# A hybrid GLA / DeltaNet block on Trainium2: the first tiles of the projection rearranged

## The chip, the cores and the metric

The kernel runs on one core of a Trainium2 chip, as one launch. The metric is the device time in microseconds of that launch, the median of several runs. The engines are PE (matmuls, with PEld for its weight loads), DVE, ACT, POOL (GpSimd) and SP, which here only issues DMAs; each has its own queue, worked off in order.

## The reference

One layer with 1024 tokens and a model width of 1024, all float32. A conditioning vector `c` gives six vectors of shift, scale and gate (adaLN); the first two act before the big projection.

```python
mod = silu(c) @ ada_w + ada_b                      # 1024 x 6144
shift1, scale1, gate1, shift2, scale2, gate2 = split(mod, 6)
h = rms_norm(x, pre_mix_w) * (1.0 + scale1) + shift1
proj = h @ w_in                                    # columns for GLA, DeltaNet, merge gates
# DeltaNet branch: d_k = l2_norm(silu(conv(proj[dk]))), beta = sigmoid(proj[beta]),
#                  g = -exp(a_log) * softplus(proj[da] + dt_bias), chunked delta rule
# GLA branch: gk = log_sigmoid(proj[lr] @ w_lr + b_lr) / 16, chunked gated linear attention
merged = sigmoid(m_a) * y_a + sigmoid(m_d) * y_d
x = x + gate1 * rms_norm(merged @ w_out, post_mix_w)
h2 = rms_norm(x, pre_mlp_w) * (1.0 + scale2) + shift2
x = x + gate2 * rms_norm(square(relu(h2 @ mlp_w1)) @ mlp_w2, post_mlp_w)
```

## The kernel before, in words

Activations are kept with channels on partitions: `hH[d]`, `hL[d]` hold channels 128 d to 128 d + 127 of all 1024 tokens. Each float32 operand is split into a high part, rounded to the matmul format, and a low part, the rest. A projection tile of 128 output columns is 8 blocks d times three products (high weight with high h, high with low, low with high) times two halves of 512 tokens: 48 matmuls into one PSUM tile of 1024 columns (pool `pm`, two tiles). A second pool, `pa`, has four banks of 512 columns for everything small.

*Start (lines 135 to 212).* SP's queue loads the eight tiles of x (128 tokens by 1024 channels each) with two small loads behind each one. `x_norm(g)` (186) takes two tiles: ACT squares with a running sum, DVE makes 1/sqrt by 13 small operations, GpSimd multiplies both tiles by it (for the last tile, DVE). The small vectors are transposed by PE into the columns `vcol` and `ccol`.

*adaLN (214 to 300).* `ada_load(p)` brings, for p = 0 to 3, the weight columns of shift and scale that belong to channel blocks 2p and 2p+1, in eight DMAs of 256 KB. The sum over the 1024 rows is shared out: the first `KPE[p]` row blocks go to PE as matmuls with one column (`ada_pe`), the rest to DVE as multiply-adds of 512 columns (`ada_part`; for p = 0 two of the blocks on GpSimd); `ada_fin` closes the sum over partitions on PE, and DVE makes shift `sh1` and scale `am1`. `modulate(p)` (301) writes `hH`, `h` (both on ACT; for p = 3 `h` on DVE) and `hL`, the difference, on DVE for one block and on GpSimd for the other. `xT`, the transposed x, comes from PE transposes, copied out of eight banks for the first four token tiles and four banks at a time for the others.

*First tiles (421 to 470).* Four rounds p: while DVE and ACT make the next two blocks, PE multiplies those that are ready with two weight tiles: the narrow tile (64 columns: low rank, beta and decay inputs, high and low part) and the first key tile of 128 columns. 14 transposes that nobody reads (`WARM`) stand ahead of the first products. From line 177 to the end of `first_tiles` the engines are strict: the class `InOrder` (27) chains each instruction of an engine behind the last one written for it. Outside of that the framework chooses the order by its own estimate of when things are ready.

*Keys (1143 to 1158).* `key_tiles` gives the first key tile and then seven more by `dense_n`, whose weights `splits` (387) prepares one ahead: ACT casts the high part, GpSimd subtracts the low part (engine G in `plan`, 378). For each tile `gdn_k` (622) does convolution, SiLU, transposes, square sums; `gates_small` (496) takes the narrow tile through DRAM and a chain of small operations to the decays; `gdn_D` (651) and `gdn_A` (659) make the decay matrix and the gram products of a head.

*The agenda (332 to 349).* `at(dt, fn)` puts work on a list to be issued dt ticks later; a tick is one of the eight blocks of a tile. The due times are numbers written by hand: transposes of keys 7 ticks after their tile, `gdn_A` 14 behind these.

Of the kernel before, what the change touches and what calls it, by code (L numbers as in the profile page):

```python
# [50 lines left out]
def block_kernel(ctx: ExitStack, tc: tile.TileContext, x, c, ada_w, ada_b, pre_mix_w, post_mix_w,  # L51
# [86 lines left out]
    smalls, o = [], 0  # L138
    for src, n in ((c, 8), (ada_b, 48), (pre_mix_w, 8), (pre_mlp_w, 8), (post_mix_w, 8), (post_mlp_w, 8), (gla_b_lr, 4),
                   (gla_onorm_w, 2), (gdn_onorm_w, 1)):  # L140
        smalls.append((vt[o:o + n, :], src.rearrange("o (r p) -> (o r) p", p=128)))
        o += n
    smalls.append((cvt, conv_w.rearrange("j (r p) -> (j r) p", p=128)))
    smalls += [(wlr[o:o + 16, :], gla_w_lr) for o in (0, 32, 64)]
    xs = []
    for i in range(NT):
        xt = t4(p="x")
        last["ld"] = DMA.dma_start(xt, x[i * 128:(i + 1) * 128, :]).ins
        xs.append(xt)
        for dst, src in smalls[2 * i:2 * i + 2]:  # L150
            with tc.issue_after(last["ld"]):
                last["ld"] = DMA.dma_start(dst, src).ins
# [3 lines left out]
    make_identity(nc, ident)  # L156
    onesR = cp.tile([128, 128], F32R, name="onesR")
# [4 lines left out]
    raw_lba = rp.tile([128, 8, 32], F32, tag="raw", name=nm("raw"))  # L162
# [16 lines left out]

    for e in engines:  # L180
        e.strict = True
# [12 lines left out]

    x_norm(0)
# [10 lines left out]
    x_norm(1)  # L206
    sigmoid(sct, ccl, V)
    V.tensor_mul(sc, ccl, sct)
    x_norm(2)
    x_norm(3)  # L210

# [11 lines left out]

    ada_load(0)
    with tc.issue_after(last["ld"]):
        for (o, c0, n) in ((0, C_LR, 16), (16, C_BETA, 8), (24, C_DA, 8)):
            DMA.dma_start(raw_lba[:, :, o:o + n], w_in[:, c0:c0 + n].rearrange("(k p) c -> p k c", p=128))
        raws0[C_DK] = load_w(w_in, C_DK, 128)
    last["ld"] = last["dma"]
    ada_load(1)  # L230

    KPE = (0, 2, 2, 1)
    WARM = 14
# [9 lines left out]
    def ada_part(p):  # L243

        for k in range(KPE[p], 8):
            r_ = araw[(p, k // 2)][:, k % 2]
            if not p and k < 2:
                a_ = t4((128, 2, 256), p="acc")
                G.tensor_scalar(a_, r_, sc[:, k:k + 1], 1.0, ALU.mult, ALU.mult)
                if k:  # L250
                    G.tensor_tensor(a_, accs[p], a_, ALU.add)
                accs[p] = a_
            elif k == (KPE[p] if p else 2):
# [895 lines left out]
    for h, ps in enumerate(key_tiles()):  # L1149
# [3 lines left out]
        elif h == 1:  # L1153
            next(gs)
# [712 lines left out]
```

## Time and profile before

| | us |
|---|---|
| median of 3 runs (lowest, highest) | 1968.18 (1964.47, 1970.18) |
| the profiled execution | 1963.2 |
| its span | 1961.5 |
| PE busy | 1921.7 |
| DVE, ACT, POOL busy | 1447.3, 801.9, 172.1 |

The page of the profile gives busy times by engine, a chain that ended last, and groups of instructions; the timeline gives single instructions with their start, their duration and, in brackets, how long the engine sat idle before them and what released it. Times in timelines count from the start of the span. All helpers record line 38, so instructions are told by their tiles: `pm` and `pa` are PSUM, `xT`, `hH`, `hL`, `h` the activations, `acc` and `araw` the adaLN sums and weights, `wH`, `wL`, `w`, `wS` weights, `cv` and `si` key convolution and its tanh, `lba` the narrow tile, `gr` the decay matrix.

### The profile page before, as it was taken

The page shows a single profiled execution, that of the slowest core. Times are in us where ns is not written, and L with a number is a line of the kernel's source. Part 1 is how long each engine was busy: PE and PEld are TensorE (multiplying, and loading weights), DVE is VectorE, ACT ScalarE, POOL GpSimd, SP SyncE. Part 2 cuts the span into 40 slices and gives each one's busy share as a digit, 9 for nine tenths or more (in the row PEclk, how much of TensorE's full clock was granted, in tenths as well). Part 3 has the DMA queues.
Part 4 walks back from the last instruction along what each step waited for, and adds up shares of the span by engine and source line. Part 5 has one row for each costly group of instructions (what it writes and reads, how often), then busy time and mean ns, then how long its engine had stood idle before and what let it go on. Part 6 is the DMA issues. An engine that isn't in the chain of part 4 may idle for free.

```text
span 1961.5 us, 26008 instructions
## 1 busy us (share of the span) xinstructions
PE 1921.7 (98%) x9894; PEld 1622.6 (83%) x9894; DVE 1447.3 (74%) x2653; ACT 801.9 (41%) x1427; POOL 172.1 (9%) x120
## 2 busy tenths in 40 slices
PE   5999999999999999999999999999999999999998
PEld 4788888889899888888888888888888888888886
DVE  7867599658769697888787434666668886787887
ACT  5554323342342333333336231247644446343333
POOL 3300100310110100000001110000012220000001
PEclk8999999999999999999999999999999999999999
DMA  9365622423222433333358785244666767452525
GB/s 295 111 211 178 202 101 84 143 65 108 60 70 76 143 111 105 116 117 114 96 162 208 184 192 124 102 131 159 205 216 214 245 228 258 158 204 66 202 97 97
DMA packets 214444, 292.24 MB, mean 149 GB/s; under 512 B 33695, under 2 KB 153966, under 8 KB 214318
## 3 DMA queue, kind: packets, MB, share of 16 engines
q1 hardware_dynamic: 174910, 243.50, 38.1%
q10 hardware_dynamic: 21760, 35.01, 5.0%
q0 software_dynamic: 17648, 12.06, 4.7%
q8 instruction: 78, 1.28, 0.3%
q14 instruction: 48, 0.39, 0.1%
HBM read 215.42 MB, written 75.11 MB: 148 GB/s over the span
## 4 chain that ended last, share of the span: by engine, by line
PE 46%; DVE 3%; DMA 1%; ACT 0%; issue 0%; DVEq 0%; ACTq 0%
PE pa L38 23%; PE pm L38 23%; DVE obT L38 1%; DVE cv L38 0%; DMA sl<-sg_d 0%; DMA os<-oa_d 0%; DVE oL L38 0%; DVE rt L38 0%; DVE si L38 0%; DVE sqt L38 0%; DVE ya L38 0%; DVE rs L38 0%; DVE sqr L38 0%; DVE yg L38 0%; DVE st L38 0%
## 5 line engine op out<-in xcount | busy, mean ns | idle before, releaser
L38 PE MATMUL pm<-hH,wH 128*128 128x512 f32 x1008 | 327.6, 405 | 0.4 <-DVE cv L38 0.4
L38 PE MATMUL pm<-hL,wH 128*128 128x512 f32 x1008 | 314.5, 393 | 0.0
L38 PE MATMUL pm<-hH,wL 128*128 128x512 f32 x1008 | 313.5, 391 | 0.1
L38 PEld LDWEIGHTS pm<-hH,wL 128*128 128x128 f32 x1008 | 189.4, 188 | 41.8 <-DVE wL L38 0.5
L38 PEld LDWEIGHTS pm<-hL,wH 128*128 128x128 f32 x1008 | 189.6, 188 | 40.9
L38 PE MATMUL pa<-w,yH 128*128 128x512 f32 x688 | 212.1, 390 | 0.0
L38 ACT CAST wH<-raw 128x1024 fp32r<-128x1024 f32 x95 | 99.1, 1051 | 270.7 <-PE pm L38 189.1
L38 PEld LDWEIGHTS pm<-hH,wH 128*128 128x128 f32 x1008 | 176.7, 190 | 26.4 <-issue 1.1
L38 DVE TENSOR_TENSOR w<-raw,w 128x512 fp32r<-128x512 f32 (+1 forms) x142 | 123.4, 872 | 49.3 <-ACT w L38 48.5
L38 PEld LDWEIGHTS pa<-w,yH 128*128 128x128 f32 x688 | 129.1, 188 | 27.2 <-DVE ya L38 0.4
L38 ACT CAST w<-raw 128x512 fp32r<-128x512 f32 (+1 forms) x143 | 98.2, 708 | 88.9 <-DVE raw L38 79.8
L38 PE MATMUL pa<-w,yL 128*128 128x512 f32 x344 | 133.9, 389 | 0.0
L38 PE MATMUL pa<-oB,w 128*128 128x512 f32 x480 | 111.4, 390 | 0.0
L38 DVE SCALAR_TENSOR_TENSOR cv<-pm,ccol,cv 128x1023 f32<-128x1023 f32 (+2 forms) x72 | 92.1, 1280 | 24.2 <-ACT cv L38 23.1
L38 DVE TENSOR_TENSOR wL<-raw,wH 128x1024 fp32r<-128x1024 f32 x72 | 88.5, 1236 | 26.9 <-ACT wH L38 26.6
L38 PEld LDWEIGHTS pa<-oB,w 128*128 128x128 f32 x480 | 89.8, 188 | 18.5 <-DVE w L38 0.2
L38 PE MATMUL pa<-oT,w 128*128 128x512 f32 x384 | 90.8, 389 | 0.0
L38 PE MATMUL pm<-oT,w 128*128 128x512 f32 x384 | 90.8, 389 | 0.0
L38 DVE TENSOR_TENSOR ya<-pa,ya 128x512 f32<-128x512 f32 x82 | 55.9, 689 | 43.3 <-PE pa L38 43.3
L38 PEld LDWEIGHTS pa<-oT,w 128*128 128x128 f32 x384 | 72.1, 188 | 14.9
L38 PEld LDWEIGHTS pm<-oT,w 128*128 128x128 f32 x384 | 72.1, 188 | 14.9
L38 PE MATMUL pm<-oH,wH 128*128 128x512 f32 x256 | 80.7, 396 | 0.0
(329 smaller groups left out, 3808.7 us busy)
## 6 DMA issues: line engine op xcount, KB each, us to landing
yL<-y_d SPq DMA_DIRECT2D x53, 512.0 KB
raw<-in_mlp_w_dram SPq DMA_DIRECT2D x23, 1024.0 KB
raw<-in_w_in_dram SPq DMA_DIRECT2D x19, 1024.0 KB
raw<-in_w_in_dram SPq DMA_DIRECT2D x34, 512.0 KB
araw<-in_ada_w_dram SPq DMA_DIRECT2D x32, 512.0 KB
raw<-in_mlp_w_dram SPq DMA_DIRECT2D x18, 512.0 KB
araw<-in_ada_w_dram SPq DMA_DIRECT2D x32, 256.0 KB
sg_d<-sig ACTq DMA_DIRECT2D x16, 512.0 KB
```

What stands on the lines that cost most here:

```text
L38: r = fn(*args, **kw)
```

## The change

- The eight tiles of x are loaded one behind the other on SP's queue; the small loads go to ACT's and GpSimd's queues. Behind x come the key weights (256 columns in place of 128), all adaLN weights, and last the narrow columns.
- The scaling of x: even tiles on DVE, odd tiles on ACT, each group of two ahead of the next squares on ACT. All eight banks serve both halves of the transposes.
- adaLN sums: PE takes 3, 2, 2, 2 row blocks in place of 0, 2, 2, 1, DVE the rest, GpSimd none. `quad` is made at the start.
- `modulate` makes `hH` and `h` on ACT; `low(d)` makes `hL[d]` on DVE alone, one block a round and the last five behind the third round.
- `first_tiles` works on two key tiles at once: `hi(p)` is 16 matmuls with the high part of h (two blocks, two tiles, high and low weight, two halves), `lo(w, d)` two matmuls with the low part. Transposes ahead of the first products: 10.
- The narrow tile follows as `lba_tile`, 32 matmuls and eight ticks, into two banks of `pa`.
- The low weights of the six other key tiles: no engine subtracts; ACT writes the negated high part, and a DMA of GpSimd's queue adds the weights to it.
- Due times: head 0's transposes still 7 ticks behind, head 1's 12; `gdn_A` 20 and 18 ticks behind these for heads 0 and 1; `gdn_D(0)` and `gdn_D(1)` at the third key tile.

```diff
-    def x_norm(g):
+    def x_sq(g):
         for i in (2 * g, 2 * g + 1):
-            A.activation(t4(p="jk"), xs[i], AF.Square, accum_out=ssq[:, i:i + 1])
+            A.activation(xT[i], xs[i], AF.Square, accum_out=ssq[:, i:i + 1])
+
+    def x_root(g):
         v = small(2, "xv")
         V.tensor_scalar(v, ssq[:, 2 * g:2 * g + 2], 1.0 / D, EPS, ALU.mult, ALU.add)
         r = rsqrt(v, 2)
-        for i in range(2):
-            (V if i and g == 3 else G).tensor_scalar(xs[2 * g + i], xs[2 * g + i], r[:, i:i + 1], 1.0, ALU.mult, ALU.mult)
+        V.tensor_scalar(xs[2 * g], xs[2 * g], r[:, 0:1], None, ALU.mult)
+        return r
+    def x_odd(g, r):
+        A.activation(xs[2 * g + 1], xs[2 * g + 1], AF.Copy, scale=r[:, 1:2])
...
+    banks = banks8()
+    x_odd(0, r0)
+    x_tr(0)
+    x_tr(1)
+    x_sq(1)
+    r1 = x_root(1)
...
+    x_odd(1, r1)
+    x_tr(2)
+    x_tr(3)
+    x_sq(2)
+    r2 = x_root(2)
+    x_odd(2, r2)
+    x_sq(3)
+    r3_ = x_root(3)
+    for d in range(8):
+        if d == 5:
+            x_odd(3, r3_)
+        A.copy(xT[d][:, :512], banks[d])
+    banks = banks8()
+    for i in range(4, 8):
+        x_tr(i)
+    wk = []
+    for i in range(2):
+        wk.append([t4((128, 8, 128), F32R, "w0", "wt") for _ in range(2)])
+        A.copy(wk[i][0], raw_k[:, :, i * 128:(i + 1) * 128])
+        V.tensor_tensor(wk[i][1], raw_k[:, :, i * 128:(i + 1) * 128], wk[i][0].bitcast(F32), ALU.subtract)
+    KPE = (3, 2, 2, 2)
...
+    ada_part(0)
     for d in range(8):
-        A.copy(xT[d][:, :512], banks[d])
+        if d % 4 == 3:
+            V.tensor_copy(xT[d][:, 512:], banks[d])
+        else:
+            A.copy(xT[d][:, 512:], banks[d])
...
+    def low(d):
+        hL[d] = t4(dt=F32R, p="hL")
+        V.tensor_tensor(hL[d], hs[d], hH[d].bitcast(F32), ALU.subtract)
...
-    plan = [(w_in, C_DK + 128, 128, 8, G)]
-    plan += [(w_in, C_DK + 256 + j * 256, 256, 8, G) for j in range(3)]
+    plan = [(w_in, C_DK + j * 256, 256, 8, None) for j in range(1, 4)]
...
     def first_tiles():
+        pk = [pmt(), pmt()]
...
+        def hi(p):
+            for d in (2 * p, 2 * p + 1):
+                for w in range(2):
+                    mm(w, 0, d, hH[d], start=(d == 0), stop=False)
+                    mm(w, 1, d, hH[d], start=False, stop=False)
+        def lo(w, d):
+            mm(w, 0, d, hL[d], start=False, stop=(d == 7))
+        ada_pe(0)
+        ada_fin(0)
+        modulate(0)
+        ada_pe(1)
+        warm(WARM)
+        for p in range(1, 4):
+            ada_part(p)
+            hi(p - 1)
+            ada_fin(p)
+            modulate(p)
+            low(p - 1)
+            if p < 3:
+                ada_pe(p + 1)
+                for w in range(2):
+                    lo(w, p - 1)
+        for d in range(3, 8):
+            low(d)
+        for w in range(2):
+            lo(w, 2)
+        hi(3)
+        for w in range(2):
+            for d in range(3, 8):
+                lo(w, d)
...
-    for h, ps in enumerate(key_tiles()):
-        gdn_k(h, ps, 7)
+    gdn_k(0, pk[0], 7, 20)
+    gdn_k(1, pk[1], 12, 18)
+    gs = gates_small(lba_tile())
+    next(gs)
+    for h, ps in enumerate(dense_n(6, h_rhs), 2):
+        gdn_k(h, ps, 7)
+        if h == 2:
+            next(gs)
+            gdn_D(0)
+        gdn_D(h - 1)
```

More of the change, by code (lines that the diff above doesn't have):

```diff
@@ L137, in block_kernel @@
     G.memset(wlr, 0.0)
[L138 to L144, printed above, removed]
     xs = []
@@ L161, in block_kernel @@
     ones = onesR.bitcast(F32)
-    raw_lba = rp.tile([128, 8, 32], F32, tag="raw", name=nm("raw"))
+    for o in (0, 32, 64):
+        G.dma_start(wlr[o:o + 16, :], gla_w_lr)
+    quad = cp.tile([128, 4, 32], F32, name="quad")
+    for a in range(0, 128, 32):
+        V.tensor_copy(quad[a:a + 32], ident[a:a + 32, a:a + 32].unsqueeze(1).to_broadcast([32, 4, 32]))
     vcol = cp.tile([128, 95], F32, name="vcol")
@@ L469, in first_tiles @@
-        for part in "lk":
-            mm(6, 1, part)
-            mm(7, 1, part)
-        for e in engines:
-            e.strict = False
+        V.tensor_tensor(wS[:, :, 32:64], raw_lba, wS[:, :, 0:32].bitcast(F32), ALU.subtract)
+        pl = [pat(), pat()]
+        for k in range(8):
+            for lo in range(2):
+                for hf in range(2):
+                    last["pe"] = T.matmul(pl[hf][:64, :], wS[:, k, :], h_rhs(k, hf, lo), start=(k == 0 and lo == 0),
+                                          stop=(k == 7 and lo == 1)).ins
+            tick()
@@ L474, in first_tiles @@
         sb = t4((64, 1024), p="lba")
         sb2 = t4((64, 1024), p="lb2")
-        A.copy(sb2, pl[0:64, :])
+        for hf in range(2):
+            A.copy(sb2[:, hf * 512:(hf + 1) * 512], pl[hf][0:64, :])
         V.tensor_copy(sb[0:32], sb2[32:64])
-        V.tensor_add(sb[0:32], sb[0:32], sb2[0:32])
-        return sb, pk
+        last["ev"] = V.tensor_add(sb[0:32], sb[0:32], sb2[0:32]).ins
+        return sb
     lrS = t4((96, 1024), F32R, p="lrS")
@@ L585, in block_kernel @@
     ssK = cp.tile([128, 64], F32, name="ssK")
-    quad = cp.tile([128, 4, 32], F32, name="quad")
-    for a in range(0, 128, 32):
-        V.tensor_copy(quad[a:a + 32], ident[a:a + 32, a:a + 32].unsqueeze(1).to_broadcast([32, 4, 32]))
     QT = 18
```

209 lines of the change are left out of this document (71 added, 138 removed).

## The prediction

> **What bounds the kernel now.** I read the page first, then the stretches of 10 us, then the waits of PE after the start, then the timeline of each engine up to 120 us.
>
> ```profile
> span 1961.5 us, 26008 instructions
> PE 1921.7 (98%) x9894; PEld 1622.6 (83%) x9894; DVE 1447.3 (74%) x2653; ACT 801.9 (41%) x1427; POOL 172.1 (9%) x120
> ...
> PE 46%; DVE 3%; DMA 1%; ACT 0%; issue 0%; DVEq 0%; ACTq 0%
> ```
>
> ```profile
> 20.00:30.00 10.00, 6.49 (x27) 4.34 (x26) 9.40 (x20) 5.76 (x12) 7.33 (x6) 0.77 1.01 258
> 30.00:40.00 10.00, 8.07 (x55) 7.35 (x54) 9.66 (x18) 4.83 (x7) 3.08 (x2) 0.84 1.10 351
> 40.00:50.00 10.00, 8.14 (x31) 5.64 (x29) 9.75 (x14) 6.57 (x6) 3.22 (x2) 0.70 1.12 337
> ...
> 70.00:80.00 10.00, 9.78 (x44) 7.76 (x42) 9.90 (x6) 2.91 (x3) 8.11 (x6) 1.00 0.69 216
> 80.00:90.00 10.00, 7.62 (x31) 6.25 (x32) 7.07 (x10) 6.42 (x24) 2.38 (x1) 0.83 0.26 73
> ```
>
> ```profile
> PE pa L38 <- DVE yn L38: 4.9, 5, 1.3
> ```
>
> PE is busy 98% of the span. The columns of the stretches are PE, PEld, DVE, ACT, POOL, then the granted clock, DMA share and GB/s. PE loses time before 60 us, where it idles and its clock is below 1, and between 80 and 90 us, at 0.83. Behind 86 us its largest wait is 4.9 us in all. The change touches only the work up to the last key tile, and the matmuls behind are the same. So its worth is how much earlier or later PE reaches one point of equal work: the start of the third key tile. All that PE must do ahead of it (narrow tile, two key tiles, eight transposes) is the same in both kernels.
>
> ```profile
> 70.10 0.61 PE L38 MATMUL pm<-hH,wH 128*128 128x512 f32 x2
> 70.55 0.62 PE L38 MATMUL pm<-hL,wH 128*128 128x512 f32 x2
> ...
> 82.39 0.66 PE L38 MATMUL pa<-ident,cv 128*128 128x128 f32 x4 [2.60 <-DVE cv L38]
> ...
> 85.62 1.20 PE L38 MATMUL pm<-hH,wH 128*128 128x512 f32 x2
> 86.62 0.76 PE L38 MATMUL pm<-hL,wH 128*128 128x512 f32 x2
> ```
>
> At full clock two matmuls start every 0.45 us, 0.227 us each. The third key tile starts at 85.62. Its first pair takes 1.0 us to the next pair instead of 0.45, so it stands as if it had started at 86.1: that is the mark. Ahead of it PE waited 2.60 us for the activated first key tile, and from 82.39 to 86.62, 4.2 us, it ran at the slow clock.
>
> **The change, part by part.** GpSimd's work is in DVE's way now.
>
> ```profile
> 30.98 0.75 DVE L38 SCALAR_TENSOR_TENSOR acc<-araw,sc,acc 128x512 f32<-128x512 f32 x1
> ...
> 33.64 3.40 DVE L38 COPY quad<-ident 32x128 f32<-32x128 f32 x4
> ...
> 41.10 2.95 DVE L38 SCALAR_TENSOR_TENSOR acc<-araw,sc,acc 128x512 f32<-128x512 f32 x1
> 43.97 1.21 DVE L38 TENSOR_TENSOR hL<-h,hH 128x1024 fp32r<-128x1024 f32 x1
> ```
>
> ```profile
> 41.14 2.36 POOL L38 TENSOR_TENSOR hL<-h,hH 128x1024 fp32r<-128x1024 f32 x1 [4.42 <-ACT h L38]
> ```
>
> The same sum takes 0.75 us alone and 2.95 us beside GpSimd's 2.36 us subtraction. A subtraction on GpSimd therefore costs DVE 2.2 us, and on DVE itself 1.21 us. So moving three of them over gains about 1 us of DVE each, and moving quad ahead frees 3.4 us of DVE before the first shift and scale. Whether that reaches PE is settled by the chain, in seven steps.
>
> *1. x.* ACT now alternates: two squares, the wait for DVE's root, one scaling.
>
> ```profile
> 7.76 1.06 ACT L38 ACTIVATE jk<-x 128x1024 f32<-128x1024 f32 x1 [1.26 <-DMA x<-in_x_dram]
> 8.72 0.19 ACT L38 ACTIVATION_READ_ACCUMULATOR jk<-x 128x1 f32 x1
> ```
>
> ```profile
> 8.94 0.17 DVE L38 TENSOR_SCALAR xv<-ssq 128x2 f32<-128x2 f32 x1 [8.94 <-ACT jk L38]
> ...
> 11.12 0.16 DVE L38 SCALAR_TENSOR_TENSOR rs<-rt,rs 128x2 f32<-128x2 f32 x1
> ```
>
> A square with its sum is 1.15 us. A root is 13 small operations from 8.94 to 11.28, 2.35 us; now it lies beside ACT's next squares, afterwards ACT stands still in it. The scaling I take as 1.06 (a pass of the same size). A group is 2.3 + 2.35 + 1.06 + 0.2 for two handovers = 5.9 us. Loading x ahead brings a tile every 1.5 us (0.52 MB at the 351 GB/s of the second stretch), faster than ACT uses them, so only the first two arrivals count: start at 5.3 as now, 0.4 us for the second tile. The nine small loads on ACT's queue must be issued before 5.3 us; I cost them at nothing, at most 1 us if the issues run longer. Four groups end at 5.7 + 23.6 = 29.3.
>
> *2. Transposes of the second half.*
>
> ```profile
> 19.69 2.05 ACT L38 COPY xT<-pa 128x512 f32<-128x512 f32 x4 [0.15 <-PE pa L38]
> ...
> 33.24 1.06 ACT L38 CAST w<-raw 128x1024 fp32r<-128x1024 f32 x1
> ```
>
> ```profile
> 26.07 6.43 PE L38 MATMUL pa<-ident,x 128*128 128x128 f32 x24 [2.69 <-POOL x L38]
> ...
> 33.56 1.73 PE L38 MATMUL pa<-ident 128*128 128x128 f32 x14
> ```
>
> The fourth pair's squares end at 5.7 + 17.7 + 2.3 = 25.7. Eight copies of 0.52 and the last scaling behind them end at 25.7 + 4.2 + 1.1 = 31.0 on ACT, and only then are all banks free. Some 24 transposes remain. The 24 of before took 6.43 with waits, the 14 at full clock 0.12 each; at half that pace they have 0.215 to 0.24. I take 0.215, 5.2 us: 36.2.
>
> *3. The first shift and scale.* ACT casts both weights, 2.1 us, to 33.1. DVE subtracts twice (1.21, as hL) to 34.3, then runs ada_part(0): 0.47 + 4 x 0.77 = 3.55, to 37.9 (0.77 is the 0.75 with its handover), then the copy that frees the fourth bank. On SP's queue the adaLN blocks of round 0 now come behind x and the 1.05 MB of key weights: 7.35 MB at 351 GB/s are 21 us behind the first bytes at 3 to 4, so 25, and DVE wants them at 34.3: covered by 9 us. Each further round's 2.1 MB take 6 us more, and rounds last 8.
>
> ```profile
> 32.44 1.28 DVE L38 COPY xT<-pa 128x512 f32<-128x512 f32 x2
> ...
> 37.45 0.47 DVE L38 TENSOR_SCALAR acc<-araw,sc 128x512 f32<-128x512 f32 x1
> ```
>
> ```profile
> 44.10 1.05 PE L38 MATMUL pa<-onesR,acc 128*128 128x1 f32 x8 [1.77 <-DVE acc L38]
> ...
> 47.30 1.06 PE L38 MATMUL pm<-hL,wS 128*64 128x512 f32 x2
> 48.15 0.63 PE L38 MATMUL pm<-hL,w 128*128 128x512 f32 x1
> ...
> 49.63 1.84 PE L38 MATMUL pa<-sc,araw 128*128 128x1 f32 x16
> ```
>
> ```profile
> 37.49 2.37 ACT L38 ACTIVATE hH<-xT,sh,am 128x1024 fp32r<-128x1024 f32 x2 [3.20 <-DVE am L38]
> ...
> 45.56 2.37 ACT L38 ACTIVATE hH<-xT,sh,am 128x1024 fp32r<-128x1024 f32 x2 [3.43 <-DVE am L38]
> ```
>
> The copy (0.64) ends at 38.6. PE's column sums ada_pe(0) then need some 20 more records of 0.115 to 0.12, 2.4 us, and the closing sums with DVE's additions 1.5 us (44.10 to 45.56): 42.5. Before, this point is 37.49. So I have the start 5 us later.
>
> *4. First round.* ada_pe(1) 1.84 to 44.3; ten transposes at 0.215 to 46.5; then hi(0), 16 matmuls. PE has had nothing but sums since 36.2, so it starts slow and stays so for the 4.2 us seen above, until 48.5: 4.8 matmuls at 0.425 (two from 47.30 to 48.15), the other 11.2 at 0.227, to 51.0. With the closing 1.5, 52.5.
>
> The row bears on a rule: the 24 transposes at 26.07 had slow clock, and by the stretches the 14 at 33.56, right behind, have 0.12 us each. Transposes count as work here. The Trainium skill, "TensorE: Matmul & The Clock Gate", Part 4, says that a transpose doesn't engage the full clock. By that rule the slow stretch would begin only at 46.5, and the sum would be 1 us more; the trace disagrees.
>
> *5. Rounds two and three.* PE: ada_pe 1.84, four low matmuls 0.9, 16 matmuls 3.63, closing 1.5, handovers 0.15: 8.0 us each, to 68.5. DVE needs 1.21 + 0.47 + 5 x 0.77 = 5.5 beside it, hidden. A round of before took 8.1 (37.49 to 45.56). Its bounds: 7.0 if sums and matmuls overlap by the waits, 9.7 if the clock drops for one 3.4 us stretch.
>
> *6. Low parts last.* After the third round DVE has six subtractions of 1.21 in a row, to 75.8; PE works beside them and ends 12 matmuls, 2.7 us, after the last: 78.5.
>
> *7. Narrow columns behind.* 32 matmuls 7.3 us, eight transposes 1.05: the third key tile at 86.9. Against the mark of 86.1 that is 0.8, say **+1 us**. The narrow matmuls cover the activation of the first key tile, so the 2.60 us wait goes.
>
> Six low parts of weights now come by adding DMA, as those of the branches do.
>
> ```profile
> DMA to landing us min/median/max: 6.7/8.9/15.3
> ```
>
> modulate(3) is four passes of 1.18 (37.49's two in 2.37) and ends at 73.2, the cast and the negation behind it at 75.3; the first DMA lands at 82 to 91 and is needed at 87.8: nothing at the median, 3 us at the longest. ACT pays a pass of 1.06 for each, hidden in a tile of 48 matmuls, 10.9 us.
>
> The profiled run's own time is 1963.2 around its 1961.5 span; +1 gives 1964. The median of three runs shown is 1968.18, so I forecast **1969**. 0.3%, 5.9 us, is about what a measurement of this kernel can tell from no change. Bounds of the steps (clock in step 5, -2 to +3.4; the DMA, 0 to 3; step 4, -2 to +1) leave this case at 1965 to 1976.
>
> **The rivals.**
>
> *The start isn't later (faster).* If ACT's three waits in the roots (7 us) don't reach PE, because x stays paced by its arrival and the copies, the first shift and scale come at 35 instead of 42.5: 7.5 us less, 1961.5. For it: DVE is 9.4 to 9.75 of 10 busy in these stretches and loses GpSimd's interference and quad. Against it: the groups are chained in the engines' fixed order.
>
> *The gates come late (slower).* The narrow tile now stands behind two key tiles.
>
> ```profile
> 72.03 3.31 DVE L38 TENSOR_TENSOR lba<-lba,lb 32x1024 f32<-32x1024 f32 x1
> 75.27 3.90 DVE L38 SCALAR_TENSOR_TENSOR cv<-pm,ccol,cv 128x1023 f32<-128x1023 f32 x3
> ...
> 105.76 3.34 DVE L38 SCALAR_TENSOR_TENSOR gr<-gr,gcC,negmask 128x128 f32<-128x128 f32 x8
> ```
>
> From its sum (75.3) to the first decay (105.8) passed 30.4 us. Afterwards the narrow matmuls end at 85.8, their copies and sums near 90, and 30.4 on is 120; decay (3.3), exponential (1.1) and product (0.75) end at 125; the gram tiles of heads 0 and 1 are due from ticks 28 and 31, 115 to 120. Four PSUM banks then hold, and PE stands 4 to 5 us with a slow clock behind, worth 2: +7 with the sum, 1975. It decides from a chain longer than some 26 us. For it: conv is queued on DVE behind the decay. Against: the due times of heads 0 and 1 were moved back by 6 and 1 ticks.
>
> *The wait at 82 stays.* The first key tile is done at 76.3; a copy and a tanh as passes of 1.1 each, taps 3.9, one tap of the other tile 1.3 and the closing pass of 1.2 end at 84.9; the transposes are due at 84.9. If DVE is behind by 2.6 us, PE waits that and runs slow again: +5, 1973, still no measurable change.
>
> **How the numbers follow.** Forecast 0.42; the wait that stays 0.10; earlier start 0.27; late gates 0.21. So faster 0.27, same 0.52, slower 0.21. The range goes 9 us to both sides, 1960 to 1978: it takes in the middle of both outer cases and leaves out their tails, some 2 in 10. The likeliest case's own is 1965 to 1976.
>
> **What would show it.** In the changed profile ACT's first hH should begin at 42.5 (35 by the faster rival), the next three 8 to 10 us apart, each DVE sum of 512 columns take 0.75, and the third key tile start at 87. PE's waits before 86 us should name the DVE sums and the roots; a wait for gr or the gram tiles between 110 and 130 us would be the slower rival. A first hH before 37 would make the forecast wrong in step 1 or 3.

## The result, and the profile after

The changed kernel takes 1987.42 us (median of 5 runs, 1985.57 to 1988.95). The kernel before, run beside it on the same chip, takes 1964.68 (5 runs, 1963.70 to 1970.18). The ratio is 1.0103, with a 95% interval of 1.0091 to 1.0116: slower by 20 us as the ratio has it, by 22.7 as the medians have it, where the forecast said 1969, 1960 to 1978. The profiled execution took 1987.42, 24.2 more than the 1963.2 of before, which lies under the lowest of these five: differences between the two traces come out a few us too large.

The page of the kernel after, its span and TensorE's busy time:

```profile
span 1985.7 us, 26066 instructions
...
PE 1927.0 (97%) x9922; PEld 1628.3 (82%) x9922; DVE 1432.1 (72%) x2657; ACT 813.9 (41%) x1440; POOL 143.2 (7%) x108
```

The waits of its TensorE (total, how often, the longest):

```profile
PE pa L38 <- DMA vt<-in_gdn_onorm_w_dram: 20.7, 1, 20.7
PE pm L38 <- DVE cv L38: 6.7, 2, 3.9
PE pa L38 <- ACT xT L38: 6.2, 1, 6.2
```

The first wait names a DMA of the small loads, and the second the key convolution, behind the first tiles. These are the two places where the time went. Three points show how much went where:

| | before | after | difference |
|---|---|---|---|
| first hH on ACT | 37.49 | 53.24 | +15.8 |
| third key tile on PE | 86.1 (the mark) | 99.89 | +13.8 |
| first sigmoid of the gates of the merge | 188.5 | 212.2 | +23.7 |

So 13.8 us are lost ahead of the third key tile, another 9.9 between it and the gates of the merge, and nothing to speak of later (23.7 of the 24.2).

**Ahead of the third key tile.** The timeline of ACT in the kernel after; ACTq rows are issues of DMAs from ACT's queue:

```profile
5.54 0.59 ACTq L38 DMA_DIRECT2D vt<-in_c_dram  x1
...
10.36 0.28 ACTq L38 DMA_DIRECT2D vt<-in_pre_mlp_w_dram  x1
13.09 0.28 ACTq L38 DMA_DIRECT2D vt<-in_post_mix_w_dram  x1
14.34 0.28 ACTq L38 DMA_DIRECT2D vt<-in_post_mlp_w_dram  x1
15.65 0.25 ACTq L38 DMA_DIRECT2D vt<-in_gla_b_lr_dram  x1
15.95 0.27 ACTq L38 DMA_DIRECT2D vt<-in_gla_onorm_w_dram  x1
16.25 0.26 ACTq L38 DMA_DIRECT2D vt<-in_gdn_onorm_w_dram  x1
16.56 1.06 ACT L38 ACTIVATE xT<-x 128x1024 f32<-128x1024 f32 x1 [12.74 <-DMA vt<-in_gla_onorm_w_dram]
...
21.22 1.15 ACT L38 ACTIVATE x<-x,rs 128x1024 f32<-128x1024 f32 x1 [2.47 <-DVE rs L38]
...
53.24 2.37 ACT L38 ACTIVATE hH<-xT,sh,am 128x1024 fp32r<-128x1024 f32 x2 [4.90 <-DVE am L38]
63.91 2.38 ACT L38 ACTIVATE hH<-xT,sh,am 128x1024 fp32r<-128x1024 f32 x2 [6.03 <-DVE am L38]
72.78 2.37 ACT L38 ACTIVATE hH<-xT,sh,am 128x1024 fp32r<-128x1024 f32 x2 [4.22 <-DVE am L38]
80.05 2.38 ACT L38 ACTIVATE hH<-xT,sh,am 128x1024 fp32r<-128x1024 f32 x2 [2.63 <-DVE am L38]
```

The nine issues themselves take 0.25 to 0.59 us each, but the first seven go out 1.3 to 2.7 us apart (only the last three follow each other in 0.3 us), and ACT does nothing else until the last one is out. The first square of x starts at 16.56. Before, it starts at 5.35.

The stretches of 10 us of the kernel after (the columns as in the prediction):

```profile
20.00:30.00 10.00, 6.56 (x34) 5.71 (x34) 5.17 (x27) 6.41 (x11) 0.00 (x0) 0.95 0.99 325
30.00:40.00 10.00, 2.12 (x6) 0.75 (x5) 5.49 (x28) 7.48 (x15) 0.00 (x0) 0.50 1.10 348
40.00:50.00 10.00, 8.47 (x46) 7.91 (x46) 7.04 (x9) 5.83 (x10) 0.00 (x0) 0.67 0.83 228
...
70.00:80.00 10.00, 9.92 (x61) 8.67 (x59) 6.63 (x15) 4.65 (x4) 0.00 (x0) 1.00 0.01 2
80.00:90.00 10.00, 8.63 (x38) 7.12 (x39) 7.51 (x9) 9.75 (x10) 2.73 (x5) 1.00 0.14 32
```

DVE, 9.4 to 9.75 of 10 busy before, has 5 to 7 now, and 6.63 against 9.90 between 70 and 80 us. The change did relieve it, and the relief is worth nothing while the chain starts 11 us late.

**Between the third key tile and the gates of the merge.** One stretch from the one point to the other, in the kernel before:

```profile
86.10:188.50 102.40, 101.96 (x521) 85.40 (x520) 67.80 (x120) 53.79 (x170) 7.73 (x5) 1.00 0.59 196
```

and in the kernel after:

```profile
99.89:212.20 112.31, 105.31 (x525) 87.40 (x524) 70.29 (x128) 58.55 (x183) 5.68 (x5) 0.97 0.73 206
```

The matmuls are the same but for a few missing records, but PE stands idle for 7.0 us (112.31 less 105.31) instead of 0.4, and it is busy 3.4 us longer at a mean clock of 0.97: together the 9.9. DVE of the kernel after shows the first idle place:

```profile
131.33 2.60 DVE L38 SCALAR_TENSOR_TENSOR cv<-pm,ccol,cv 128x1023 f32<-128x1023 f32 x2 [2.23 <-ACT cv L38]
138.51 2.19 DVE L38 SCALAR_TENSOR_TENSOR gr<-gr,gcC,negmask 128x128 f32<-128x128 f32 x8 [4.58 <-DMA gr<-gc_d]
140.61 1.28 DVE L38 SCALAR_TENSOR_TENSOR cv<-pm,ccol,cv 128x1021 f32<-128x1021 f32 x1
```

and PE, which needs the convolved tile's PSUM:

```profile
142.03 1.19 PE L38 MATMUL pm<-hH,wH 128*128 128x512 f32 x2 [3.94 <-DVE cv L38]
...
160.90 0.70 PE L38 MATMUL pm<-hH,wH 128*128 128x512 f32 x2 [2.75 <-DVE cv L38]
```

Two taps of a convolution are done. Then the first decay stands at the head of DVE's queue and waits 4.58 us for its load of `gr`, with the third tap behind it and PE behind that. The narrow sum ends at 108.9 and the first decay starts at 138.5, 29.6 us later; before it was 30.4. The gates come 32.7 us later than before (138.5 against 105.8), the key tiles only 13.8.

The wait has a second side, the load itself. SP issues it in the kernel before and in the kernel after at

```profile
99.67 0.36 SPq L653 DMA_DIRECT2D gr<-gc_d  x1
```

```profile
128.79 0.35 SPq L667 DMA_DIRECT2D gr<-gc_d  x1
```

Before, the decay at 105.76 doesn't wait, so that its load took at most 6.1 us; now it takes until 138.5, 9.7 us. For most of that time the DMA engines have next to nothing to do (the last columns, 0.04 busy and 17 GB/s):

```profile
130.00:136.00 6.00, 6.00 (x36) 5.27 (x35) 2.56 (x2) 3.68 (x7) 1.54 (x1) 1.00 0.04 17
```

With the 6.1 us of before it would have landed at 134.9, and DVE, free from 133.9 on, would have waited 1 us and not 4.58 (an estimate from these rows). The slow load doesn't come with the new order: where a first decay waits for its load, in old orders (e2, e9, e12, e18) and new ones, it took 8.8 to 10.3 us, once 6.7 (e4). What makes it slow isn't shown.

The second wait of PE, 2.75 us at 160.90, comes by ACT's queue: DVE has stood idle for 5.0 us when the first tap reaches it at 156.84, and ACT had the exponentials of two decays and a held store ahead of that tap.

### The profile page after: what moved, and what is told of

Read it like the earlier page. It is cut to its first block, busy times and chain, and to the rows that moved or that the text cites. A ratio compares the mean times of both kernels' runs of the same rounds, so it can differ in the third digit from the quotient of the medians.

```text
span 1985.7 us, 26066 instructions
## 1 busy us (share of the span) xinstructions
PE 1927.0 (97%) x9922; PEld 1628.3 (82%) x9922; DVE 1432.1 (72%) x2657; ACT 813.9 (41%) x1440; POOL 143.2 (7%) x108
## 5 line engine op out<-in xcount | busy, mean ns | idle before, releaser
L38 PE MATMUL pm<-hH,wH 128*128 128x512 f32 x992 | 322.6, 405 | 6.7 <-DVE cv L38 6.7
L38 PE MATMUL pm<-hL,wH 128*128 128x512 f32 x992 | 309.5, 392 | 0.0
L38 PE MATMUL pm<-hH,wL 128*128 128x512 f32 x992 | 309.0, 392 | 0.1
L38 PEld LDWEIGHTS pm<-hL,wH 128*128 128x128 f32 x992 | 186.5, 188 | 40.6
```

The source lines that it names most:

```text
L38: r = fn(*args, **kw)
```

## The experiments

Each kernel ran beside the kernel before on one chip; the ratio is to that. The theory was that two things cost the time: the small loads on ACT's queue, and gates that come late against the key tiles. The rivals are named with each run. Kernels that ran on different chips are compared by their ratios. One trace is good to some 2 us: six kernels with the same code ahead of the first hH (after, e3, e4, e5, e10, e16) have it between 52.3 and 54.2.

| kernel | ratio to before (95%) | first hH | third key tile | first decay | first sigmoid |
|---|---|---|---|---|---|
| before | | 37.5 | 86.1 | 105.8 | 188.5 |
| after | 1.0103 (1.0091 to 1.0116) | 53.2 | 99.9 | 138.5 | 212.2 |
| e1 small loads on SP | 1.0064 (1.0039 to 1.0089) | 45.2 | 92.6 | 131.5 | 204.0 |
| e2 before, small loads on ACT | 1.0053 (1.0033 to 1.0073) | 46.7 | 94.5 | 118.8 | 200.3 |
| e3 due times later | 1.0141 (1.0119 to 1.0163) | 54.0 | 100.5 | 152.2 | 216.7 |
| e4 low weights on DVE | 1.0148 (1.0124 to 1.0172) | 54.2 | 101.4 | 141.8 | 218.4 |
| e6 e1, squares ahead | 1.0045 (1.0031 to 1.0059) | 37.5 | 84.9 | 124.5 | 197.2 |
| e7 small loads on GpSimd | 1.0055 (1.0036 to 1.0074) | 43.1 | 89.3 | 128.6 | 200.7 |
| e8 e7, squares ahead | 1.0022 (1.0009 to 1.0035) | 39.6 | 85.9 | 124.5 | 197.0 |
| e9 before, quad first | 1.0009 (0.9998 to 1.0020) | 34.7 | 85.0 | 109.6 | 192.6 |
| e10 decays behind conv | 1.0106 (1.0088 to 1.0124) | 52.3 | 98.4 | 137.2 | 213.7 |
| e12 before, quad first, decays behind conv | 0.9987 (0.9976 to 0.9998) | 35.0 | 84.4 | 108.2 | 186.5 |
| e15 before, gates delayed | 1.0033 (1.0021 to 1.0045) | 37.8 | 86.4 | 113.6 | 195.1 |
| e16 e10, stores on GpSimd | 1.0122 (1.0089 to 1.0155) | 54.2 | 101.6 | 139.5 | 206.6 |

### The small loads

**e2, the kernel before with one part of the change alone.** The nine small loads go to ACT's queue, behind x:

```diff
+    A.strict = True
+    for dst, src in vts:
+        A.dma_start(dst, src)
```

> The kernel before with one part of the change alone: the nine small vector loads on ACT's queue, behind x (the other small loads stay on SP's queue, behind the last two x tiles). Theory: ACT's first square begins at 15 us or later instead of 5.35; since GpSimd scales here and ACT need not wait for the roots, eight squares of 1.15 end near 26 instead of 19.5, the first hH moves from 37.5 to 43 or 44 and the time by 5 to 7 us. Rival (issuing a small load costs ACT 0.3 us each, 3 us in all, under the wait for x): no change within 2 us.

1977.80 us against 1968.79: 9 us, more than expected. By the traces the third key tile is 8.4 us late, and another 3.4 us go behind it, where a decay waits 4.7 us for its load. ACT of this kernel:

```profile
7.96 0.58 ACTq L38 DMA_DIRECT2D vt<-in_c_dram  x1
...
15.09 0.28 ACTq L38 DMA_DIRECT2D vt<-in_post_mlp_w_dram  x1
15.40 0.31 ACTq L38 DMA_DIRECT2D vt<-in_gla_b_lr_dram  x1
...
16.36 1.06 ACT L38 ACTIVATE jk<-x 128x1024 f32<-128x1024 f32 x1 [12.60 <-DMA vt<-in_gla_onorm_w_dram]
```

Here the issues begin 2.4 us later than in the kernel after, yet both are free of the hold at about the same moment: from 15.4 on they follow each other in 0.3 us. An estimate from the rows: x is 4.19 MB, at 355 GB/s (10 to 20 us of the kernel after) 11.8 us behind its first bytes at 3 to 4. That fits a hold that ends about when x has been taken in; no run has fewer small loads, so what their number does isn't shown. Busy DMA engines alone don't make the hold: in the kernel after they are as busy from 15 to 20 us (1.01, 314 GB/s, x and the weights behind it), and the last three issues follow in 0.3 us. Nor is ACT alone held: SP's next issue behind the eight tiles of x goes out at 11.66 there, but at 5.78 in e7, where ACT issues none.

**e1, the kernel after with the small loads on SP's queue, two behind each tile of x, as before.**

> The changed kernel with one part undone: the nine small vector loads go back to SP's queue, two behind each of the first x tiles. Theory (the small loads hold ACT's queue until x has passed): ACT's first square begins near 5.5 us instead of 16.56, the first hH near 42.5 instead of 53.2, and the whole is about 11 us faster, some 1976 against 1987.4. Rival (the new order of square, root and scaling on ACT is what came late, and the small loads only overlapped it): first hH moves by under 3 us, the time by under 3 us.

1980.59 against 1968.79, by the ratio 7.7 us of the expected 11 back. The first square starts at 5.68, but the second at 8.74 instead of 6.9: between the tiles of x, the small loads hold up x itself.

**e7, the kernel after with the small loads on GpSimd's queue, behind ident.**

```diff
-        A.dma_start(vt[o:o + n, :], src.rearrange("o (r p) -> (o r) p", p=128))
+        G.dma_start(vt[o:o + n, :], src.rearrange("o (r p) -> (o r) p", p=128))
```

> The changed kernel with the nine small loads on GpSimd's queue, behind the identity, instead of ACT's. Theory (an issue on ACT stands behind the transfers of x that SP's queue has put in, GpSimd's own queue does not hold ACT): ACT's first square near 5.5, x one tile every 1.5 us, first hH near 42.5, time 9 to 11 us less than 1987.4. Rival (any small load behind x lands late, whatever the queue, and the transposes of the vectors hold DVE and PE): first hH later than 46.

1976.07 against 1965.11; the ratio falls from 1.0103 to 1.0055, which is 9.4 us. GpSimd of this kernel issues the nine in a row, from

```profile
1.78 0.72 POOL L38 DMA_DIRECT2D vt<-in_c_dram  x1
...
6.15 0.52 POOL L38 DMA_DIRECT2D vt<-in_gdn_onorm_w_dram  x1
```

while x is loading, and is not held. Its ACT:

```profile
5.65 1.06 ACT L38 ACTIVATE xT<-x 128x1024 f32<-128x1024 f32 x1 [1.86 <-DMA x<-in_x_dram]
...
6.93 1.06 ACT L38 ACTIVATE xT<-x 128x1024 f32<-128x1024 f32 x1
...
43.05 2.37 ACT L38 ACTIVATE hH<-xT,sh,am 128x1024 fp32r<-128x1024 f32 x2 [5.25 <-DVE am L38]
```

The first hH comes at 43.05, where the prediction's steps 1 to 3 said 42.5 for a start without a hold. The theory stands, and so does the sum of these steps, apart from the one term.

**e6 and e8, squares ahead.** In e1's and e7's kernels ACT makes the next group's squares before it scales a tile, so that DVE's root lies beside them (2.4 us of waiting a group in the timeline of after).

```diff
-    x_odd(0, r0)
-    x_tr(0)
-    x_tr(1)
     x_sq(1)
     r1 = x_root(1)
+    x_odd(0, r0)
+    x_tr(0)
+    x_tr(1)
```

> The changed kernel with the small loads on SP's queue and, beside that, each group's squares ahead of the scaling of the group before, so that ACT squares while DVE makes a root. Theory (square, root and scaling in a fixed row on ACT are a second loss of the start, 2.35 us in each of three groups): first hH near 39 instead of 45.2 in the kernel with the small loads alone undone, time 5 to 6 us less than its 1980.6. Rival (behind x the transposes and the sums, not ACT, set the start): first hH within 1.5 us of 45.2, time within 2 us.

> The changed kernel with the small loads on GpSimd's queue and each group's squares ahead of the scaling of the group before. Theory (two separate losses of the start): first hH at 36 to 38 instead of 43.05 with the loads alone moved, time 5 to 7 us less than its 1976.1. Rival (the start is then set by the sums and their weights' arrival): first hH above 40, under 3 us.

1974.83 for e6 and 1971.65 for e8. By the ratios that is 3.7 us under e1, less than expected, and 6.5 under e7. First hH comes 7.7 and 3.5 us earlier; e8's 39.6 falls short of the 36 to 38 expected. The waits for the roots did reach PE: the prediction's faster rival supposed that they don't.

In e8 the third key tile starts at 85.9, level with before, and still the kernel is 0.22% slower: everything that is left is lost behind that point.

### The gates

**e3, due times of the first heads later** (decays due at ticks 34 to 37, gram products at 37 to 45), and **e5, the first two heads' key transposes later** (ticks 11 and 14).

> The changed kernel with later due times only: decays of heads 0 to 3 at ticks 34 to 37 instead of 24 to 36, their gram products at 37, 39, 41 and 45. Theory (DVE's convolution stands behind a decay that waits for the gates, and PE behind the convolution): the waits of PE of 3.9 and 2.75 us at 142 and 161 us and the slow clock behind them go, 6 to 9 us faster, near 1980. Rival (the adding DMAs for the low weights load the queues and delay weights and decays): the waits stay, time within 2 us of 1987.4.

> The changed kernel with the transposes of the first two key tiles four and two ticks later (11 and 14 ticks instead of 7 and 12; their gram products keep ticks 27 and 30), so that the narrow tile's last matmuls and its copies on ACT stand ahead of the square sums of the first key head. Theory (late gates): the narrow tile's sum ends at 102 to 104 us instead of 108.9, the first decay starts 5 us earlier than 138.5, PE's wait of 3.9 us at 142 shrinks to 1 or less, time 3 to 6 us less than the changed kernel's 1987.4. Rival (the wait comes from the convolution's own place, not from the gates): the decay starts earlier but the wait stays, time within 2 us.

1994.64 and 1986.86: 7 us worse, and no change. In e3 DVE makes four decays in a row (8.5 us from 152.18), later ones then wait for buffers of `gr` that come free late, and PE waits 6.3 and 4.5 us for a convolution: the same wait at another place. e5 moves the narrow sum by 1.2 us only, so it decides nothing.

**e4, no adding DMAs:** the six key tiles' low weights are subtracted on DVE.

```diff
-    plan = [(w_in, C_DK + j * 256, 256, 8, None) for j in range(1, 4)]
+    plan = [(w_in, C_DK + j * 256, 256, 8, V) for j in range(1, 4)]
```

> The changed kernel with the low weights of the six key tiles subtracted on DVE (1.22 us each) instead of negated on ACT and added by DMA. Theory (late gates): the waits at 142 and 161 us stay, time within 2 us of 1987.4. Rival (adding DMAs are the cause): the waits go, 5 us or more faster.

1996.66, 9 us worse, with waits of 5.8 and 5.2 us. The rival falls: the waits are there without the adding DMAs, too, and these relieve DVE. How much of the 9 us is DVE's added work isn't told.

**e9 and e12, the kernel before with quad at the start**, and with the decays issued behind the convolution as well:

```diff
-        with V.behind():
+        with V.behind(), tc.issue_after(last["ev"]):
...
-        at(4 if h else 8, lambda: decay(gr, h))
+        at(4 if h else 9, lambda: decay(gr, h))
```

> The kernel before with one part of the change alone: quad is made at the start. Theory (the copies of quad, 3.4 us beside GpSimd, held DVE right ahead of the first shift and scale): first hH 2.5 to 3.5 us earlier than 37.49, time 2 to 4 us less than the kernel before. Rival (DVE's next sums and GpSimd's subtractions take the place): no difference beyond 1.5 us.

> The kernel before with quad at the start and the decays behind the convolution (head 0's one tick later). With quad alone the first hH came 2.8 us earlier and the time did not fall, and PE waited 3.0 us for a convolution behind a decay. Theory: without that wait the gain shows, 3 to 5 us less than the kernel before. Rival (the gain is lost elsewhere): within 1.5 us of it.

e9 gains 2.8 us at the first hH (34.73) and loses it again: 1967.54, ratio 1.0009 (0.9998 to 1.0020). The first decay, at 109.61, waits 5.0 us for its load, issued at 99.43, and PE waits 3.0 at 113.13 for the tap behind it. Its stretch from the third key tile to the gates of the merge is 107.6 us, 5.2 over before's, with the narrow columns where they always were: a slow load ahead of a tap is enough. With that order turned round, e12 keeps the gain, though its load is as slow (98.81 to 108.2): the stretch is 102.1 us, the time 1965.30 against 1968.36. This is the one version here that beats the kernel before, by 2.6 us as the ratio has it, and its interval only just leaves out no change.

**e10 and e11, the same order in the kernel after and in e8.**

> The changed kernel with the decays of heads 0 and 1 one tick later (25 and 26 in place of 24 and 25) and every decay chained behind the last convolution tap written before it: on DVE the whole convolution of the key tile then stands ahead of the first decay. Theory (the convolution's third tap waits behind a decay that waits for the load of gr, and the tile's bank with it): PE's wait of 3.9 us at 142 goes, its second wait shrinks, the slow clock goes, 5 to 8 us less than 1987.4. Rival (late gates hold PE through the PSUM banks of the gram products, whatever stands where on DVE): PE's waits stay above 3 us in sum, and the time within 2 us.

> The changed kernel with all three: small loads on GpSimd's queue, squares ahead, decays behind the convolution. If the three losses add: 1987.4 less 11, less 6, less 6, near 1964, even with the kernel before (1965 to 1968). Rival (what the start gains is lost again because the gates come late against PE): 1970 or more.

1989.20 and 1974.79: nothing gained, and e11 is 3 us over e8. The decays are out of the way, but the wait moves. ACT of e10:

```profile
148.73 0.61 ACTq L690 DMA_DIRECT2D X_d<-a  x1
154.87 0.53 ACTq L691 DMA_DIRECT2D a_d<-a  x1
155.44 0.28 ACT L38 ACTIVATE ktok<-pa 128x128 f32<-128x128 f32 x1 [6.13 <-DMA X_d<-a]
...
156.46 1.13 ACT L38 ACTIVATE cv<-pm,ccol 128x1024 f32<-128x1024 f32 x1
```

and its PE:

```profile
161.75 1.19 PE L38 MATMUL pm<-hH,wH 128*128 128x512 f32 x2 [7.95 <-DVE cv L38]
```

ACT can't issue a head's third store of 128 KB until 6.1 us after the second (for the later heads 3.1 us), and the first tap of the next convolution stands behind that store.

**e13, e14, e15: how late the gates come, moved by itself.** e13 is e8 with the narrow tile's PSUM copied by DVE instead of ACT. e14 is e8 with the narrow matmuls put ahead of the key tiles' last low products. e15 is the kernel before with eight copies on GpSimd between narrow sum and gates:

```diff
+        for _ in range(4):
+            G.tensor_copy(sb2[0:32], sb[0:32])
+            G.tensor_copy(sb[0:32], sb2[0:32])
```

> The kernel with the small loads on GpSimd's queue and the squares ahead, in which the narrow columns' two PSUM halves are now copied by DVE and not by ACT. In its trace the narrow products end at 85.5, but ACT, busy with the key tiles' squares, copies the halves only at 91.4 and 92.4, and the narrow sum ends at 95.0; DVE stands idle from 87.9. So far the stage from the third key tile's first matmul to the first sigmoid of the gates of the merge has taken 102.4 us where the first decay came 20 us behind that matmul (before), 104 to 109 where it came 26 behind, 111 to 115 where it came 39 behind. Theory (what costs is how far the gates come behind the key tiles): narrow sum about 4 us earlier, first decay 35 behind, the stage 108 to 110 instead of 111.1, time 1 to 3 us under that kernel's 1971.65. Rival (a fixed price of the new order, whatever the gates do): within 1 us of 1971.65.

> The same kernel (small loads on GpSimd's queue, squares ahead) with the narrow columns put ahead again: their 32 matmuls run before the last twenty low products of the two key tiles, ACT copies them and DVE adds them there. Theory (lateness of the gates): narrow sum near 85 instead of 95, first decay near 114.5; the third key tile has nothing left to run beside the evacuation of the first and starts 2 to 5 us later (near 89), so the decay comes 25 behind it and the stage takes 104 to 108: first sigmoid 193 to 197, against 197.0, and time 1966 to 1971. Rival (the evacuation that the narrow columns covered costs as much as the late gates): 1971 to 1975, with a wait of 4 us or more ahead of the third key tile.

> The kernel before with nothing changed but a delay between the narrow sum and the gates: GpSimd copies the sum back and forth eight times, some 10 us by its rows (the second key tiles' low weights on GpSimd may move by some us too). Theory (lateness of the gates is the price of the second half of the loss): first decay near 115, 29 behind the third key tile, PE waits for the conv behind the decays again, stage 105 to 109 instead of 102.4, time 3 to 7 us over before's. Rival (the gates have slack of 10 us, and the loss comes from the other things that the change put behind the first tiles): within 1.5 us of before's.

e15 came out as the theory had it: 1973.77 against 1968.15, in the stretch from the third key tile on

```profile
86.39:195.10 108.71, 103.53 (x524) 86.35 (x523) 73.69 (x127) 56.24 (x179) 11.60 (x8) 0.98 0.56 186
```

5.2 us of idle time and a mean clock of 0.98, where before has 0.4 and 1.00. Late gates alone, in the old order of work, cost some 6 us. Of the idle time 3.4 us is a wait of PE for the gates' own small tiles, which its fixed order has at that place; 1.8 is the tap behind the decay, which doesn't wait for its load here. In the kernel after PE waits 0.3 us for such small tiles, so e15 shows that late gates cost something, but not by which way they do so there.

The other two are misses. e13 (1973.33) has the decay 2.2 us earlier and gains nothing. e14 is 12 us worse than e8 (1983.98): the narrow sum ends at 82.7, 12 us earlier than in e8, but the first decay comes at 126.4, 1.9 later than there. So the 30 us from sum to decay aren't the length of that chain alone. Its small operations stand in the order of issue behind convolutions, which are later in e14 (third key tile 87.7), and an earlier sum is of no use to them. In both kernels the longest wait (6.3 us in e13, 12.9 in e14) has ACT held at a store again, for 7.4 and 6.6 us; in e14 a decay that waits for its load stands ahead of the taps as well.

**e16, e17, e18: a head's three stores on GpSimd's queue** instead of ACT's, in e10, in e13 and in e12.

```diff
-            ST.dma_start(xv[0], a3[0:64, :, 0:64])
+            G.dma_start(xv[0], a3[0:64, :, 0:64])
```

> The kernel after with the decays behind the conv (e10), and each head's three stores of its gram products (X_d twice, a_d) issued from GpSimd's queue instead of ACT's. With the decays out of the conv's way PE still waited 8.0 us at 161.75, for a conv whose first tap ACT began only at 156.46: ACT's queue issued X_d at 148.73 and the next store, a_d, at 154.87, and the tap stood behind that (for the later heads the same two issues are 3.1 us apart). Theory (late gates bunch the heads' decays and stores, and ACT is held at the issues with the tap behind them): the wait falls to 2 to 4 us, first sigmoid 3 to 6 earlier than 213.7, time 1983 to 1986 against 1989.2. Rival (the stores hold nothing; the tap is late because its matmuls or the transposes ahead of it are): the wait stays over 6 us, time within 2 us of 1989.2.

> The kernel of e13 (small loads on GpSimd's queue, squares ahead, narrow copies on DVE) with the same three stores on GpSimd's queue. There PE waited 6.29 at 146.79; ACT's X_d went out at 132.47, its a_d at 139.89, 7.4 us on, the first tap at 141.49. Theory: that wait falls by 3 to 5 us, time 1968 to 1971 against 1973.33. Rival: within 1.5 us of 1973.33.

> The kernel of e12 (before, quad at the start, decays behind the conv) with the same three stores on GpSimd's queue. There PE waits 0.3 us in all between the third key tile and the gates of the merge, so theory and rival both give no change: within 1.5 us of its 1965.3, some 3 us under before. A gain over that would say that the stores on ACT cost something later too; a loss, that GpSimd's queue is the worse place (its subtractions of the low weights then stand behind the stores).

In e16 the wait of 7.95 us is gone, and the stretch is

```profile
101.55:206.60 105.05, 102.40 (x518) 85.33 (x517) 73.84 (x131) 61.02 (x186) 18.05 (x23) 0.98 0.78 236
```

105.05 us, 10.2 less than e10's 115.26 and 2.7 over before's, with gates as late as in the kernel after. So with the decays behind the taps and the stores off ACT's queue, late gates cost little there. The time doesn't follow: 1991.04 (1983.87 to 1993.55), against 1989.20 for e10. GpSimd and DVE of e16, further on, show one place where it was given back:

```profile
370.35 4.49 POOL L38 TENSOR_SCALAR_AFFINE_SELECT X<-X 128x1024 f32<-128x1024 f32 x3 [124.86 <-DVE X L38]
374.81 2.39 POOL L38 TENSOR_TENSOR zm<-zm,b 128x1024 f32<-128x1024 f32 x1
```

```profile
377.23 3.21 DVE L38 TENSOR_TENSOR_SCAN b<-smask,zm 128x1024 f32<-128x1024 f32 x1 [5.60 <-POOL zm L38]
```

The solve now ends earlier, and its selects stand on GpSimd's queue ahead of the product that the scan waits for. PE waits 2.7 us there and runs at 0.96 of the clock from 380 to 420; the scan starts at 377.23, where e10's starts at 377.09. Another 3.1 us were lost ahead of the stretch: e16's third key tile starts at 101.6, e10's at 98.4, with the same code before it.

e17 is worse than e13 (1981.09, waits 8.1 and 1.8). It has the decays ahead of the taps again: a decay waits 7.7 us for its load, which SP issues at 138.27, behind the load of a head's `a` at 137.65; by its place, that one waits for the store of `a` of 133.91. e18 changes nothing (1967.65, ratio 1.0006, 0.9993 to 1.0018), 3.7 us over e12 by the ratios, whose intervals just overlap.

## Why the prediction was wrong

**Step 1 failed**, in this sentence: "The nine small loads on ACT's queue must be issued before 5.3 us; I cost them at nothing, at most 1 us if the issues run longer." They cost 9 to 11 us: 10.2 at the first hH and 9.4 in the time by e7, 9.2 and 9.0 by e2. The start it assumed (5.3) was 16.56. The working took the issue of a DMA for a short operation on ACT's queue, from its own duration, and left out that the issue can be held while x is being taken in. e2 shows it by itself, and e7 shows that the rest of steps 1 to 3 adds up: 43.05 against 42.5.

One page speaks to this. The Trainium skill, "DMA: Bandwidth & Descriptors", section "Issuing engines are not separate DMA queues", says that starting DMAs from several engines saves only the time that it takes to initiate them, "which is usually small relative to the DMA itself". The trace agrees that the queues aren't separate: ACT's issues and SP's hold each other up (SP's next one at 11.66, or at 5.78 without ACT's). The trace disagrees on the small price, for a compute engine: ACT lost 11 us to nine loads.

The other steps, by the kernel after and e7:

- Step 1, a group: 5.7 us apart (21.22, 26.91, 32.61) against 5.9. Right.
- Steps 2 and 3: transposes and first hH late by the same 10.1 to 10.7 us as x. Right in sum, with some luck: in e7 the column sums `ada_pe(0)` behind the copies took 3.4 us (37.90 to 41.28) where the sum had 2.4, and began 0.7 us earlier than it had them.
- Step 4: 10.7 us (53.24 to 63.91) against 10.0. PE of the kernel after:

```profile
53.18 3.55 PE L38 MATMUL pa<-sc,araw 128*128 128x1 f32 x16
56.59 2.38 PE L38 MATMUL pm<-ident 128*128 128x128 f32 x10
58.62 4.38 PE L38 MATMUL pm<-hH,w 128*128 128x512 f32 x16
...
63.64 1.93 PE L38 MATMUL pa<-sc,araw 128*128 128x1 f32 x16
```

  The column sums took 0.22 us each at the slow clock, where the sum had 0.115 from rows at full clock: 1.7 us mis-sized. The same row of 16 takes 1.93 at 63.64. Part of that came back in the matmuls behind. The 4.2 us at the slow clock are misread, too: the kernel before has its granted clock at 0.99 until 83.5 and at 0.50 from there to 86.9, which is 3.4 us.
- Step 5: 8.9 and 7.3 us against 8.0 each, 16.1 together against 16.0. That is luck: a round is 7.3 (in e7 both are), near the step's lower bound, and in the first one here the clock fell (16 matmuls took 5.2 us from 66.46 on, 3.65 in the next round).
- Step 6: from the fourth hH to the last low product 10.6 us against 10.0. Right.
- Step 7: 9.3 us against 8.35, with a wait of 0.9 for the activated tile. The 2.60 us wait is gone, as predicted. The adding DMAs never hold PE, though three of them took 15 us to land in the median, longer than the 8.9 that stood in the sum.

Steps 4 to 7 together are 46.65 us against 44.4, 2.2 too few. Without the hold, the third key tile would have come within 3 us of the prediction (e7: 89.3 against 86.9).

**The second error** is the 9.9 us behind the third key tile. "The gates come late" had this place, with the convolution on DVE behind the decay, and it was priced at 6 us and given a chance of 0.21. Lateness should have been part of the sum, since the profile before had the 30.4 us and the order on DVE; the slow load of `gr` was not to be read there, where it took at most 6.1 us. Its place was right, DVE's queue at the first decay (138.5; without the 13.8 us of delay, inside the 110 to 130 named). Its bank argument is not what the kernel after shows: PE waits for the convolved tile, not for gram products. And it is not one wait. Once the gates are late, the decays of heads 1 and 2 come at once (two in a row at 144.43), with their loads, stores and products in between three convolutions, and whichever in-order queue carries both holds the convolution: in after DVE's at the first wait and ACT's at the second, ACT's in e10, both in e13.

What is shown: the small loads (e2, e7); that late gates cost some 6 us by themselves in the old order (e15), and a slow load ahead of a tap about as much without them (e9 against e12); that DVE's and ACT's queues are where PE's convolution is held, since the stretch returns to within 2.7 us of before when both are cleared (e16). What stays open: how the 9.9 us divide between late gates and the slow load, what makes the load slow, and whether the narrow columns can stand behind two key tiles without loss in the end. The version that would join e8's start with e16's order and keep GpSimd free at 370 us wasn't tried.

## What to carry to other kernels

A DMA that is issued from a compute engine's queue can cost that engine not the issue's own duration but the time until the queue takes it (here 11 us for nine loads of 0.3 to 0.6), so count it as a wait where large transfers are under way, and put it on a queue with nothing urgent behind it. When a change moves a producer back, list what its late consumers will stand in front of on each in-order queue, and price each; here, moving them on one queue moved the wait to the next. When an engine waits for a load, look at the load's issue as well: it may be slow and not late. A relieved engine (DVE here, from over 9 of 10 to 5 to 7) is worth nothing until the first link of its chain is on time.

## What was new about the hardware

- ACT's issues were held while x was being loaded on SP's queue (355 GB/s): nine loads from 5.54 to 16.25 us, the last three of them in 0.6 us with the DMA engines still at 1.01. SP's own next issue was held with them (11.66, against 5.78 in e7). GpSimd's, in the same time, go out every 0.5 us (1.78 to 6.15).
- A store of 128 KB on ACT is mostly held 3.1 to 3.4 us behind the one before it, and 6.1 to 7.4 us in e10, e13 and e14. Loads of `gr` were under way in these, but in the kernel after as well (3.2 us), so they alone don't explain it.
- The same 512 KB load of `gr` took 8.8 to 10.3 us in most traces and at most 6.1 in the kernel before; in the kernel after, most of this passed with the DMA engines 0.04 busy.
- From 48.44 to 56.6 us PE is nearly always busy with sums of one column. They begin at the full clock (granted 1.00 from 46 to 49 us), it falls to 0.50 at 49.4, and their pace is 0.22 us from there on: 7 us of them don't bring the full clock back. Whether it fell for them or for the gaps of PE just before (47.3 to 48.44) isn't shown. The trace doesn't tell whether the ten transposes behind them bring it, or the first matmuls.
- Transposes alone did bring it just before: from 41.44 to 46.28 PE runs nothing else, and the granted clock goes from 0.50 to 1.00 at 46.
